# Banded output blocks moved ahead of their gates and stored ungated, with a second seven-product pair

## The chip, the cores and the metric

The kernel runs on one core of a Trainium2 chip. The metric is the device time of one execution in microseconds (us); less is better. The core has five engines with a queue of instructions each: PE multiplies matrices, ACT (ScalarE) and DVE (VectorE) work elementwise, POOL (GpSimd) mostly issues DMAs here, SP issues the loads of the weights. Each engine runs its instructions in an order that is fixed when the kernel is built; an instruction that waits holds up all that stand behind it on its engine. SBUF is the on-chip memory, PSUM the eight banks that PE writes its sums to, DRAM the memory outside.

## The reference, cut to what matters

One layer of a decoder trunk on 256 tokens of width 2048, all in float32. Three sub-steps matter: the projection of the gates, the two attention branches with an output projection each, and the merge.

```python
c_q, c_kv, k_r, q_s, k_s, v_s, gates = jnp.split(h @ w_in, offsets, axis=-1)
...
o_a = mla_attention(q_nope, q_rope, k_nope, k_rope, v)     # 16 heads, dense causal
o_b = swa_attention(q_s, k_s, v_s, swa_sinks, rel_table)   # 32 heads, banded, window 128
g = jax.nn.sigmoid(gates).reshape(B, S, 2, D_MODEL)
merged = g[:, :, 0] * (o_a @ w_o_mla) + g[:, :, 1] * (o_b @ w_o_swa)
y = merged @ w_out
```

The B branch (banded attention) ends in `sigmoid(gB) * (o_b @ w_o_swa)`; `gB` and `o_b @ w_o_swa` are two products of 256 x 2048 by 2048 x 2048. After the mixer come a norm, a gated convolutional feed-forward part and another norm, which the change does not touch.

## The kernel before, in words

**Products.** A float32 product is made of three passes on PE: operands are split into a high and a low part, and high by high, high by low and low by high are added up in PSUM (`mm3`, lines 174 to 177). Activations lie split in SBUF: the normed input in the eight tiles `xt` (family a, read through `XH` and `XL`), the banded attention's output in the eight tiles `ot` (family b, `OH` and `OL`). Weights come from DRAM through SP into raw tiles of 128 x 1024, and are split by `convert` (lines 134 to 145): ACT casts the high part `whi`, DVE subtracts for the low part `wlo`. Four such pairs of tiles form a ring, so the conversions run up to four tiles ahead of PE.

**A plain block.** `gemm` makes 256 tokens by 512 columns: eight weight tiles of two k-tiles each, for both halves of the tokens (t = 0, 1). After each weight tile `tick()` is called, which emits whatever was set for that step with `at(step, ...)`; so side work is spread over the steps of the main products.

**A pair.** `pair_gemm` makes two blocks (1024 columns) at once, from eight units of two k-tiles each. A unit `p` (plain) is eight products of 128 x 128 by 128 x 512. A unit `s` (`seven`) makes the same 2 x 2 x 2 block product with seven products, in the manner of Strassen and Winograd: it needs sums of the activations (`token_sums`) and sums of the weights (four subtractions of 512 columns on DVE), and its weight rows are loaded by POOL, not SP. Four sums `c` gather in four PSUM banks, and four others `q` in the other four; `kind` says which four are which. After the last unit `s` the `q` banks are combined into four tiles `d` in SBUF (`first_sums`, `more_sums`); to finish, `c` has to be added to `d`.

**The order around the change.** Behind the banded attention and the two latent projections come, one after another: gate block 0 (`gate_b(0)`, columns from `C_GB`), banded output block 0 (`out_b(0)`), gate blocks 1 and 2 as a pair (`gate_pair(1)`, order "psppspsp"), then output block 1, gate block 3, output blocks 2 and 3. `gate_b` leaves tanh of half of the gate in SBUF tiles `tb`; `out_b` multiplies (tanh + 1) by its PSUM sum on DVE (line 707) and POOL stores the gated product to `yb_d` in DRAM. The eight units of the latent attention (`mla_unit`) begin 26 steps after the gate pair and run beside output block 3 and the A gates; their outputs go into the b family again (`at_`), once the banded outputs are no longer needed. Then come the four blocks of the A gates, stored to `ta_d`.

**The merge** (lines 938 to 958) runs beside the four blocks of `wo_a`: POOL loads the stored A gate into `lta` (three buffers) and the gated B product into `lyb` (two buffers); DVE multiplies (tanh + 1) by the PSUM sum, adds the B product, and PE transposes the result (`m_cols`).

Other names: `stg` are four staging tiles of 128 x 512; `pacc` has four PSUM banks, `pss` and `pst` two each; `gr` are the two buffers for the rows that POOL loads, `gta` and `gtb` the sums of the weights.

Of the kernel before, what the change touches and what calls it, by code (L numbers as in the profile page):

```python
# [11 lines left out]
F32 = mybir.dt.float32  # L12
F32R = mybir.dt.float32r
# [3 lines left out]
ALU = mybir.AluOpType  # L17
AX = mybir.AxisListType

P = 128  # L20
D = 2048
S = 256
NT = 2
KT = D // P
# [17 lines left out]
def trunk_layer(ctx, tc, x, x_cols_in, conv_cols_in, g_mix_post, g_ffn_post, w_in, w_q, w_kv,  # L42
                sinks, rel, wo_a, wo_b, w_out, w_up, w_down, rope_tab, strip_sel, out):
    nc = tc.nc
    vec, act, pe, pool = nc.vector, nc.scalar, nc.tensor, nc.gpsimd
# [13 lines left out]
    def sb(pl, shape, name, dt=F32, tag=None, bufs=None):  # L59
        return pl.tile(shape, dt, name=name, tag=tag or name, **({"bufs": bufs} if bufs else {}))  # L60
# [41 lines left out]
    cnt = [0]  # L102
# [52 lines left out]
    now = [0]  # L155

    def at(t, *fs):
        steps[max(t, now[0])].extend(fs)
# [20 lines left out]
    def gemm(xh, xl, w, k0, nk, c0, n, split=None, extra=None, ps=None):  # L179

        kc = 1024 // n if n in (256, 512) else 2
        acc = new_acc("g", ps)
        todo = []
        cuts = list(range(0, nk, kc)) + [nk]
        for ci, (k, ke) in enumerate(zip(cuts[:-1], cuts[1:])):
            kk = ke - k
            src = w[(k0 + k) * P:(k0 + k + kk) * P, c0:c0 + n].rearrange("(a p) n -> p a n", p=P)
            hi, lo = wchunk(src, [kk, n], *(extra or {}).get(ci, ()))
            for j in range(kk):
                kt = k + j  # L190
# [85 lines left out]
    def token_sums(g, a, m, hi, lo):  # L276

        vec.tensor_tensor(a, g[:, 0:512], g[:, 512:1024], op=ALU.add)
        a11, a21, a12, a22 = (a[:, i * P:(i + 1) * P] for i in range(4))
        m1, m2, m3, m4 = (m[:, i * P:(i + 1) * P] for i in range(4))  # L280
        vec.tensor_tensor(m1, a21, a22, op=ALU.add)
        vec.tensor_tensor(m3, a11, a21, op=ALU.subtract)
        vec.tensor_tensor(m2, m1, a11, op=ALU.subtract)
        vec.tensor_tensor(m4, a12, m2, op=ALU.subtract)
        split_to(hi, lo, m)
        return [[x[:, i * P:(i + 1) * P] for x in (hi, lo)] for i in range(4)]
# [71 lines left out]
    xt = [slot("a", p) for p in range(8)]  # L358
# [139 lines left out]
    ot = [slot("b", p) for p in range(8)]  # L498
    OH, OL = pair_view(highs(ot)), pair_view(lows(ot))
# [113 lines left out]
    for g in range(4):  # L613
        acc = gemm(XH, XL, w_in, 0, KT, C_QS + 512 * g, 512)[0] if g else acc_q0
        swa_q(g, acc)
        b = now[0]
# [10 lines left out]
    stg = lambda name, n=512: sb(lpool, [P, n], name, tag="stg", bufs=STG)  # L627
# [36 lines left out]
    acc, _ = gemm(XH, XL, w_in, 0, KT, 0, 512)  # L664
# [25 lines left out]

    ta_d = dram.tile([4, NT, P, 512], F32, name="ta_d")
    yb_d = dram.tile([4, NT, P, 512], F32, name="yb_d")
    x2_d = dram.tile([NT, P, D], F32, name="x2_d")

    def gate_b(j):
        acc, _ = gemm(XH, XL, w_in, 0, KT, C_GB + 512 * j, 512)
        tb = []
        for t in range(NT):
            g = stg(f"tb{j}_{t}")
            act.activation(g, acc[t], AF.Tanh, scale=rh[:, t:t + 1])  # L700
            tb.append(g)
        return tb

    def out_b(j, tb, ps=None):
        acc, _ = gemm(OH, OL, wo_b, 0, KT, 512 * j, 512, ps=ps)
        for t in range(NT):
            vec.scalar_tensor_tensor(tb[t], tb[t], 1.0, acc[t], op0=ALU.add, op1=ALU.mult)
            pool.dma_start(yb_d[j, t], tb[t])

    es1.close()  # L710
    esb.close()
    esg, pg = open_pool("pg")
    xs = {}

    def x_sums(u):
        st = sb(pg, [P, 1024], f"xs{u}", F32R)
        a, m = (sb(pg, [P, 512], f"x{n}{u}", tag="x" + n, bufs=1) for n in "am")
        xs[u] = token_sums(xt[u].bitcast(F32), a, m, st[:, 0:512], st[:, 512:1024])

    def g_place():  # L720
        both = sb(pg, [P, D], f"gr{cnt[0]}", tag="gr", bufs=2)
        return both[:, 0:1024], both[:, 1024:2048]

    def gate_pair(j):
        d = [stg(f"tb{j + i}_{t}") for t in range(NT) for i in range(2)]
        c = pair_gemm("g", w_in, 0, C_GB + 512 * j, GATE_ORDER, lambda k, t: (XH(k)[:, t * P:(t + 1) * P], XL(k)[:, t * P:(t + 1) * P]),
                      lambda u: xs[u], 0, d, g_place, lambda: [sb(pg, [P, 1024], f"gt{n}{cnt[0]}", tag="gt" + n, bufs=2) for n in "ab"])
        def finish_gate(i):
            vec.tensor_tensor(d[i], d[i], c[i], op=ALU.add)
            act.activation(d[i], d[i], AF.Tanh, scale=rh[:, i // 2:i // 2 + 1])  # L730

        for n_, i in enumerate((0, 2, 1, 3)):
            at(now[0] + n_, lambda i=i: finish_gate(i))
        return [d[0], d[2]], [d[1], d[3]]

    tb = {0: gate_b(0)}
    for u in range(GATE_ORDER.count("s")):
        at(now[0] + 3 * u, lambda u=u: x_sums(u))
    out_b(0, tb[0], (pss, "s"))
    tb[1], tb[2] = gate_pair(1)  # L740
    esg.close()


    es2, p2 = open_pool("p2")
    CQH, CQL = pair_view(cqh), pair_view(cql)
    CKH, CKL = pair_view([ckh]), pair_view([ckl])
    ath, atl = [], []
    AH, AL = pair_view(ath), pair_view(atl)
    wq3 = w_q.rearrange("(k p) (h c) -> p k h c", p=P, c=192)
    xr_of = {}  # L750
# [133 lines left out]
        at(t0 + 6, lambda: pt(0), lambda: pt(1))  # L884
        at(t0 + 7, lambda: pv(0), lambda: pv(1))

    b = now[0] + 26
    for u in range(8):
        if u % 4 == 0:
            q_rope8(u // 4, b + 4 * u)  # L890
        mla_unit(u, b + 4 * u)

    for j in range(1, 4):
        out_b(j, tb[j], (pss, "s") if j == 1 else None)
        if j == 1:
            tb[3] = gate_b(3)
    at_ = [slot("b", p) for p in range(8)]
    ath[:], atl[:] = highs(at_), lows(at_)
    for j in range(4):
        acc, _ = gemm(XH, XL, w_in, 0, KT, C_GA + 512 * j, 512)  # L900
        for t in range(NT):
            g = stg(f"ta{j}_{t}")
# [35 lines left out]
    def merge_loads(j):  # L938
        ld = []
        for t in range(NT):  # L940
            a = sb(p4, [P, 512], f"lta{j}_{t}", tag="lta", bufs=3)
            b = sb(p4, [P, 512], f"lyb{j}_{t}", tag="lyb", bufs=2)
            pool.dma_start(a, ta_d[j, t])
            pool.dma_start(b, yb_d[j, t])
            ld.append((a, b))
        return ld

# [376 lines left out]

RING = 4
GATE_ORDER = "psppspsp"
B_ORDER = "pppsppspsp"
PAIR_ORDER = ("psppsppsppsp", "ppsppsppsppp")
XCUT = [0, 1, 2, 3, 4, 6, 8, 10, 12, 14, 16]
# [73 lines left out]
```

## Time and profile before

| | |
|---|---|
| time, median of 3 runs | 1468.54 us (1467.81 to 1469.31) |
| the profiled execution | 1470.05 us, of which the span is 1468.3 us |
| PE busy, share of the span | 99% |
| DVE, ACT, POOL | 73%, 57%, 4% |
| granted clock of PE | 0.998 of full speed |

The profile is of one execution. A row of the timeline or of a group names the line of the kernel, the engine, the operation and the tiles (out<-in); in a group the last figures are minimum, median and maximum in ns. "Idle before" in square brackets says how long the engine stood before the instruction and what released it. A product of 128 x 512 shows 0.39 us, but products are pipelined, so that one begins every 0.23 us. Some product records can be missing from a trace, so counts of products are a few per cent low.

### The profile page before, as it was taken

How to read it: one execution, taken by the hardware profiler on the slowest of the kernel's cores; microseconds unless marked ns; L12 is line 12 of the kernel's file. 1: busy time of each engine (PE TensorE's matmuls, PEld its weight loads, DVE VectorE, ACT ScalarE, POOL GpSimd, SP SyncE). 2: the span in 40 equal slices, each digit the busy share in tenths (PEclk: the TensorE clock that was granted, in tenths of full speed). 3: DMA queues.
4: the chain of work that ended last, by engine and by line, in shares of the span. 5: the costliest groups of instructions: out<-in, count | busy, mean ns of one | idle time of the engine just before them, and what ended most of it. 6: DMA issues, size and time to landing. Idle time of an engine off the chain costs nothing.

```text
span 1468.3 us, 20938 instructions
## 1 busy us (share of the span) xinstructions
PE 1456.9 (99%) x7576; PEld 1244.8 (85%) x7576; DVE 1067.2 (73%) x1881; ACT 830.5 (57%) x1372; POOL 64.9 (4%) x113
## 2 busy tenths in 40 slices
PE   9999999999999999999999999999999999999997
PEld 7888888888888888888888888888888888888886
DVE  7688896745667665555699976778776687677775
ACT  7588874543555554444566655555454565555453
POOL 0011110000000000000000000000000000000000
PEclk9999999999999999999999999999999999999999
DMA  8755376466655559756766666665656666667573
GB/s 297 211 164 167 108 259 192 162 212 200 191 156 160 164 163 334 226 184 212 225 205 185 188 193 193 187 187 187 218 174 213 198 187 189 187 197 233 163 237 129
DMA packets 149909, 287.60 MB, mean 196 GB/s; under 512 B 18428, under 2 KB 29597, under 8 KB 149677
## 3 DMA queue, kind: packets, MB, share of 16 engines
q1 hardware_dynamic: 141312, 256.80, 56.5%
q0 software_dynamic: 8400, 29.41, 6.4%
q8 instruction: 59, 0.97, 0.3%
q14 instruction: 46, 0.37, 0.1%
q10 hardware_dynamic: 92, 0.05, 0.0%
HBM read 277.79 MB, written 8.44 MB: 195 GB/s over the span
## 4 chain that ended last, share of the span: by engine, by line
PE 97%; DVE 2%; ACT 1%; issue 0%; DMA 0%; DVEq 0%; ACTq 0%
PE accg L175 13%; PE accg L177 13%; PE accg L176 13%; PE ub L1147 10%; PE ua L1147 10%; PE ua L1151 5%; PE ub L1151 5%; PE cd L177 2%; PE cd L175 2%; PE cd L176 2%; PE cdb L175 1%; PE cdb L177 1%; PE cdb L176 1%; PE mpo L875 1%; PE cg L176 1%; PE cg L177 1%
## 5 line engine op out<-in xcount | busy, mean ns | idle before, releaser
L144 DVE TENSOR_TENSOR wlo<-raw,whi 128x1024 fp32r<-128x1024 f32 (+2 forms) x476 | 576.3, 1214 | 282.5 <-ACT whi L143 275.2
L143 ACT CAST whi<-raw 128x1024 fp32r<-128x1024 f32 (+2 forms) x476 | 494.7, 1043 | 427.5 <-PE accg L177 172.3
L175 PE MATMUL accg<-whi,ahl 128*128 128x512 f32 (+1 forms) x480 | 187.9, 392 | 0.0
L177 PE MATMUL accg<-whi,ahl 128*128 128x512 f32 (+1 forms) x480 | 185.6, 387 | 0.0
L176 PE MATMUL accg<-wlo,ahl 128*128 128x512 f32 (+1 forms) x480 | 184.8, 385 | 0.0
L1147 PE MATMUL ua<-ahl,whi 128*128 128x512 f32 x640 | 154.6, 391 | 0.0
L1147 PE MATMUL ub<-ahl,whi 128*128 128x512 f32 x640 | 154.6, 391 | 0.0
L175 PE MATMUL accg<-whi,bhl 128*128 128x512 f32 x378 | 148.2, 392 | 0.0
L177 PE MATMUL accg<-whi,bhl 128*128 128x512 f32 x378 | 147.4, 390 | 0.0
L176 PE MATMUL accg<-wlo,bhl 128*128 128x512 f32 x378 | 147.3, 390 | 0.0
L1147 PEld LDWEIGHTS ub<-ahl,whi 128*128 128x128 f32 x640 | 117.5, 188 | 22.9 <-ACT cc L1045 0.2
L1147 PEld LDWEIGHTS ua<-ahl,whi 128*128 128x128 f32 x640 | 117.6, 188 | 22.7
L177 PEld LDWEIGHTS accg<-whi,ahl 128*128 128x128 f32 x480 | 90.1, 188 | 18.0
L176 PEld LDWEIGHTS accg<-wlo,ahl 128*128 128x128 f32 x480 | 90.3, 188 | 15.6
L175 PEld LDWEIGHTS accg<-whi,ahl 128*128 128x128 f32 x480 | 90.3, 188 | 15.5
L1151 PEld LDWEIGHTS ub<-ahl,wlo 128*128 128x128 f32 x640 | 82.2, 191 | 3.2
L1151 PEld LDWEIGHTS ua<-ahl,wlo 128*128 128x128 f32 x640 | 82.2, 191 | 3.1
L1151 PE MATMUL ua<-ahl,wlo 128*128 128x256 f32 x640 | 83.7, 283 | 0.0
L177 PEld LDWEIGHTS accg<-whi,bhl 128*128 128x128 f32 x378 | 71.0, 188 | 14.8
L176 PEld LDWEIGHTS accg<-wlo,bhl 128*128 128x128 f32 x378 | 71.0, 188 | 14.5
L1151 PE MATMUL ub<-ahl,wlo 128*128 128x256 f32 x640 | 83.2, 283 | 0.0
L175 PEld LDWEIGHTS accg<-whi,bhl 128*128 128x128 f32 x378 | 71.0, 188 | 14.3
(545 smaller groups left out, 2218.9 us busy)
## 6 DMA issues: line engine op xcount, KB each, us to landing
raw<-in_ffn_w_up_dram SPq DMA_DIRECT2D x176, 512.0 KB, 4.5
raw<-in_w_in_dram SPq DMA_DIRECT2D x105, 512.0 KB, 4.5
raw<-in_ffn_w_down_dram SPq DMA_DIRECT2D x68, 512.0 KB, 4.5
raw<-in_w_o_swa_dram SPq DMA_DIRECT2D x32, 512.0 KB, 4.4
raw<-in_w_o_mla_dram SPq DMA_DIRECT2D x32, 512.0 KB, 4.5
raw<-in_w_out_dram SPq DMA_DIRECT2D x32, 512.0 KB, 4.1
bias<-strip POOLq DMA_DIRECT2D x16, 256.0 KB, 4.4
raw<-in_mla_w_q_up_dram SPq DMA_DIRECT2D x32, 128.0 KB, 2.8
```

The lines of the kernel that those rows point to most:

```text
L143: act.copy(hi[:, a:b], raw[:, a:b])
L144: vec.tensor_tensor(lo[:, a:b], raw[:, a:b], hi[:, a:b].bitcast(F32), op=ALU.subtract)
L175: pe.matmul(o, ah, bh, start=start, stop=False)
L176: pe.matmul(o, ah, bl, start=False, stop=False)
L177: pe.matmul(o, al, bh, start=False, stop=stop)
L875: pe.matmul(o, w(t), p_[:, c], start=n == 0, stop=n == 5)
L1147: pe.matmul(acc[i], hi[:, c], hn[p][:, j * 512:(j + 1) * 512], start=p + j == 0, stop=stop)
L1151: pe.matmul(acc[i][:, 0:256], lo[:, c], hn[p][:, j * 512:j * 512 + 256], start=False, stop=False)
```

## The change

The banded output blocks no longer wait for their gates, since both go to DRAM by themselves: the output blocks ungated to `yb_d`, the tanh of the gates to a new `tb_d`. The order becomes output blocks 0 and 1 (plain), output blocks 2 and 3 as a pair (`out_pair(2)`), gate blocks 0 and 1 as a pair (`gate_pair(0)`), and then gate blocks 2 and 3 (plain) beside the latent attention, which begins 2 steps after the gate pair instead of 26. The `at_` tiles are taken right behind the gate pair.

Both pairs have three seven-product units. For them the sums of the activations are made for three tiles of `ot` and three of `xt`, spread over the steps of output blocks 0, 1 and the pair; the third sum of `xt` lies in the place of the first of `ot`.

The gate pair uses banks of the other kind than before (kind 1). In the output pair `d` is stored to `yb_d` first; then each `c` is copied by ACT to one of two buffers `yc` and added to what is stored by a DMA with an accumulating write.

The merge loads three tiles per token half (gate B, output B, gate A) with two buffers each, and multiplies (tanh + 1) by output B on DVE five steps into each block.

```diff
+    tb_d = dram.tile([4, NT, P, 512], F32, name="tb_d")
...
     def gate_b(j):
...
             act.activation(g, acc[t], AF.Tanh, scale=rh[:, t:t + 1])
-            tb.append(g)
-        return tb
-
-    def out_b(j, tb, ps=None):
-        acc, _ = gemm(OH, OL, wo_b, 0, KT, 512 * j, 512, ps=ps)
+            pool.dma_start(tb_d[j, t], g)
+
+    def out_b(j):
+        acc, _ = gemm(OH, OL, wo_b, 0, KT, 512 * j, 512, ps=(pss, "s") if j == 1 else None)
         for t in range(NT):
-            vec.scalar_tensor_tensor(tb[t], tb[t], 1.0, acc[t], op0=ALU.add, op1=ALU.mult)
-            pool.dma_start(yb_d[j, t], tb[t])
+            o = stg(f"yb{j}_{t}")
+            act.copy(o, acc[t])
+            pool.dma_start(yb_d[j, t], o)
...
+    def pair_sums(name, into, tiles, u):
+        st = sb(pg, [P, 1024], f"{name}{u}", F32R, tag="os0" if u == 2 and name == "xs" else f"{name}{u}")
+        a, m = (sb(pg, [P, 512], f"{name}{n}{u}", tag="x" + n, bufs=1) for n in "am")
+        into[u] = token_sums(tiles[u].bitcast(F32), a, m, st[:, 0:512], st[:, 512:1024])
...
     def gate_pair(j):
...
-                      lambda u: xs[u], 0, d, g_place, lambda: [sb(pg, [P, 1024], f"gt{n}{cnt[0]}", tag="gt" + n, bufs=2) for n in "ab"])
+                      lambda u: xs[u], 1, d, g_place, g_temps)
...
             act.activation(d[i], d[i], AF.Tanh, scale=rh[:, i // 2:i // 2 + 1])
+            pool.dma_start(tb_d[j + i % 2, i // 2], d[i])
...
+    def out_pair(j):
+        d = [stg(f"yu{j + i}_{t}") for t in range(NT) for i in range(2)]
+        c = pair_gemm("o", wo_b, 0, 512 * j, OUT_ORDER, lambda k, t: (OH(k)[:, t * P:(t + 1) * P], OL(k)[:, t * P:(t + 1) * P]),
+                      lambda u: os_[u], 0, d, g_place, g_temps)
+        for i in range(4):
+            pool.dma_start(yb_d[j + i % 2, i // 2], d[i])
+
+        def finish_out(i):
+            e = sb(pg, [P, 512], f"yc{i}", tag="yc", bufs=2)
+            act.copy(e, c[i])
+            pool.dma_start(yb_d[j + i % 2, i // 2], e, accum_op=ALU.add)
+
+        for i in range(4):
+            at(now[0] + i // 2, lambda i=i: finish_out(i))
+
+    for n_, u in ((6, 0), (9, 1), (12, 2)):
+        at(now[0] + n_, lambda u=u: pair_sums("os", os_, ot, u))
+    for n_, u in ((10, 0), (14, 1), (20, 2)):
+        at(now[0] + n_, lambda u=u: pair_sums("xs", xs, xt, u))
+    out_b(0)
+    out_b(1)
+    out_pair(2)
+    gate_pair(0)
     esg.close()
+    at_ = [slot("b", p) for p in range(8)]
+    ath, atl = highs(at_), lows(at_)
...
-    b = now[0] + 26
+    b = now[0] + 2
...
-    for j in range(1, 4):
-        out_b(j, tb[j], (pss, "s") if j == 1 else None)
-        if j == 1:
-            tb[3] = gate_b(3)
-    at_ = [slot("b", p) for p in range(8)]
-    ath[:], atl[:] = highs(at_), lows(at_)
+    for j in range(2, 4):
+        gate_b(j)
...
     def merge_loads(j):
         ld = []
         for t in range(NT):
-            a = sb(p4, [P, 512], f"lta{j}_{t}", tag="lta", bufs=3)
-            b = sb(p4, [P, 512], f"lyb{j}_{t}", tag="lyb", bufs=2)
-            pool.dma_start(a, ta_d[j, t])
-            pool.dma_start(b, yb_d[j, t])
+            a, g, b = (sb(p4, [P, 512], f"l{n}{j}_{t}", tag="l" + n, bufs=2) for n in ("ta", "tb", "yb"))
+            for dst, src in ((g, tb_d), (b, yb_d), (a, ta_d)):
+                pool.dma_start(dst, src[j, t])
+            at(now[0] + 5, lambda b=b, g=g: vec.scalar_tensor_tensor(b, g, 1.0, b, op0=ALU.add, op1=ALU.mult))
             ld.append((a, b))
...
 GATE_ORDER = "psppspsp"
+OUT_ORDER = "psppspsp"
```

More of the change, by code (lines that the diff above doesn't have):

```diff
@@ L696, in gate_b @@
         acc, _ = gemm(XH, XL, w_in, 0, KT, C_GB + 512 * j, 512)
-        tb = []
         for t in range(NT):
@@ L712, in trunk_layer @@
     esg, pg = open_pool("pg")
[L713 to L718, printed above, removed]
+    xs, os_ = {}, {}
+    def pair_sums(name, into, tiles, u):
+        st = sb(pg, [P, 1024], f"{name}{u}", F32R, tag="os0" if u == 2 and name == "xs" else f"{name}{u}")
+        a, m = (sb(pg, [P, 512], f"{name}{n}{u}", tag="x" + n, bufs=1) for n in "am")
+        into[u] = token_sums(tiles[u].bitcast(F32), a, m, st[:, 0:512], st[:, 512:1024])
     def g_place():
@@ L722, in g_place @@
         return both[:, 0:1024], both[:, 1024:2048]
+    g_temps = lambda: [sb(pg, [P, 1024], f"gt{n}{cnt[0]}", tag="gt" + n, bufs=2) for n in "ab"]
     def gate_pair(j):
@@ L730, in finish_gate @@
             act.activation(d[i], d[i], AF.Tanh, scale=rh[:, i // 2:i // 2 + 1])
[L732 to L740, printed above, removed]
+            pool.dma_start(tb_d[j + i % 2, i // 2], d[i])
+        for i in range(4):
+            at(now[0] + i // 2, lambda i=i: finish_gate(i))
+    def out_pair(j):
[8 more added lines that the diff above has]
+            pool.dma_start(yb_d[j + i % 2, i // 2], e, accum_op=ALU.add)
+        for i in range(4):
+            at(now[0] + i // 2, lambda i=i: finish_out(i))
[7 more added lines that the diff above has]
+    gate_pair(0)
     esg.close()
+    at_ = [slot("b", p) for p in range(8)]
+    ath, atl = highs(at_), lows(at_)
     es2, p2 = open_pool("p2")
@@ L746, in trunk_layer @@
     CKH, CKL = pair_view([ckh]), pair_view([ckl])
-    ath, atl = [], []
     AH, AL = pair_view(ath), pair_view(atl)
```

## The prediction

> **What bounds the kernel.** I read the page's head first, then its chain of waits.
>
> ```profile
> span 1468.3 us, 20938 instructions
> PE 1456.9 (99%) x7576; PEld 1244.8 (85%) x7576; DVE 1067.2 (73%) x1881; ACT 830.5 (57%) x1372; POOL 64.9 (4%) x113
> PE 97%; DVE 2%; ACT 1%; issue 0%; DMA 0%; DVEq 0%; ACTq 0%
> ```
>
> PE is busy for 99% of the span and makes 97% of the chain. Only fewer products, or a PE stall, can move the time. The second view is a table of stretches around the change; its columns are PE, PEld, DVE, ACT, POOL busy us (count), granted clock, DMA share, GB/s.
>
> ```profile
> 200.00:220.00 20.00, 20.00 (x92) 16.52 (x91) 20.00 (x50) 10.68 (x18) 2.51 (x5) 1.00 0.84 297
> 220.00:240.00 20.00, 20.00 (x90) 16.56 (x89) 12.90 (x15) 9.53 (x11) 0.00 (x0) 1.00 0.70 206
> 240.00:260.00 20.00, 20.00 (x89) 16.22 (x88) 14.16 (x16) 9.55 (x10) 2.17 (x4) 1.00 0.61 202
> 260.00:280.00 20.00, 20.00 (x89) 16.42 (x88) 11.92 (x12) 11.86 (x13) 0.00 (x0) 1.00 0.21 68
> 300.00:320.00 20.00, 20.00 (x90) 16.57 (x89) 10.57 (x10) 7.39 (x7) 1.10 (x2) 1.00 0.73 228
> ```
>
> PE has no hole and full clock, so there is no stall here to win back. A busy PE can still step slowly, so the third view is PE's timeline: first product of banded output block 0, first of the old gate pair, three marks in its first seven-product unit, the two steps that a late tile spoiled, and the first product behind the pair.
>
> ```profile
> 220.91 0.39 PE L175 MATMUL accg<-whi,bhl 128*128 128x512 f32 x1
> 242.67 0.39 PE L175 MATMUL cg<-whi,ahl 128*128 128x512 f32 x1
> ...
> 248.11 0.39 PE L175 MATMUL cg<-whi,ahl 128*128 128x512 f32 x1
> ...
> 250.89 0.39 PE L175 MATMUL qg<-whi,xs 128*128 128x512 f32 x1
> ...
> 251.60 0.40 PE L175 MATMUL qg<-whi,xs 128*128 128x512 f32 x1
> ...
> 252.98 0.39 PE L175 MATMUL cg<-whi,ahl 128*128 128x512 f32 x1
> 253.28 0.50 PE L176 MATMUL cg<-wlo,ahl 128*128 128x512 f32 x1
> 253.62 0.39 PE L177 MATMUL cg<-whi,ahl 128*128 128x512 f32 x1
> ...
> 284.68 0.39 PE L175 MATMUL accg<-whi,bhl 128*128 128x512 f32 x1
> ```
>
> A plain block is 96 products (16 k-tiles, 2 token halves, 3 products each) in 242.67 - 220.91 = 21.76 us: 0.2267 us a product, 2.72 us a weight tile (12 products). The durations of 0.39 overlap and are not the step.
>
> **Part 1, the products removed.** A plain unit of a pair is 2 x 2 x 2 x 3 = 24 products, a seven-product unit 21. Before, one pair (gates 1-2) has three such units; after, two pairs have six. So 9 products go, at most 9 x 0.2267 = 2.04 us. The old pair shows what such units really return: it lasts 284.68 - 242.67 = 42.01 us, two plain blocks 43.52, a gain of 1.51. The missing 0.53 is 0.19 at the late tile (252.98 to 253.62 is 0.64 for two steps of 0.227) and 0.34 in slightly slower steps with the summed operand. **I take -1.51**; bounds -2.04 and 0.
>
> **Part 2, VectorE's extra work.** The second pair adds, per seven-product unit, four subtractions and 1.5 more tile conversions, then four final sums, and three token sums.
>
> ```profile
> L232 DVE TENSOR_TENSOR gta<-gr x3: 678/685/692, 207.5 to 249.7; 128x512 f32<-128x512 f32 x3
> 240.15 1.05 ACT L143 CAST whi<-gr 128x1024 fp32r<-128x1024 f32 x1 [1.67 <-PE accg L177]
> 241.23 1.23 DVE L144 TENSOR_TENSOR wlo<-gr,whi 128x1024 fp32r<-128x1024 f32 x1 [1.49 <-ACT whi L143]
> ```
>
> That is 3 x (4 x 0.685 + 1.5 x 1.23) + 4 x 0.68 + 3 x 2.5 = 24 us; 2.5 for a token sum is an estimate (two additions of 0.685 and four on a quarter of the width). The stretch from banded block 0 to the end of the gate pair becomes 2 x 21.76 + 2 x 42.0 = 127.5 us. DVE has there what the first four stretches hold (59.0), 47.5 us of plain work at 10.57 per 20 (25), and the 24: 108 of 127.5, 0.85. In 200 to 220 it was full and PE did not stall. Cover in time: the low half above ends at 242.46 and its first product is at 248.11, so a DVE delay of 5.65 us is hidden in plain units. ACT ends at 241.20, 6.9 ahead. Cost 0; without that cover each 1.23 us conversion would be a stall. Gating only moves: the product of 1.28 for two tiles (L707 below) leaves the output blocks, ACT's copies (0.57) take its place, and eight products of 0.64 go to the merge.
>
> **Part 3, POOL's loads.** The even and odd rows of seven-product units go through two buffers and POOL's queue.
>
> ```profile
> 200.65 0.56 POOL L227 DMA_DIRECT2D gr<-in_w_in_dram  x1 [0.30 <-POOL bhl L605]
> ...
> 243.35 1.14 POOL L708 DMA_DIRECT2D yb_d<-tb  x2 [40.54 <-DVE tb L707]
> 244.55 0.54 POOL L227 DMA_DIRECT2D gr<-in_w_in_dram  x1
> 245.08 0.54 POOL L228 DMA_DIRECT2D gr<-in_w_in_dram  x1
> 242.37 1.28 DVE L707 SCALAR_TENSOR_TENSOR tb<-tb,accg 128x512 f32<-128x512 f32 x2
> 249.66 0.69 DVE L232 TENSOR_TENSOR gta<-gr 128x512 f32<-128x512 f32 x1 [1.77 <-DMA gr<-in_w_in_dram]
> ACT whi L143 <- DMA raw<-in_ffn_w_down_dram: 40.5, 23, 4.8
> ```
>
> Before, two of three loads ran 40 us ahead; the third left when a buffer came free, DVE stood 1.77 us at its subtraction with a conversion queued behind, and PE lost the 0.19 above. After, four loads are of that kind; one is in the 1.51, and the gate pair's first two are wanted more than 20 us after their buffers come free. **I take +0.2**; bounds 0 and 3.2 each (a wait of 4.8, the longest for a load in the table of waits, 3.0 more than 1.77).
>
> **Part 4, the accumulate chain, where the change adds waits.** At the end of the output pair (call it T; 284.68 in the old pair) four partial blocks are stored, the other four are copied by ACT into two buffers, and each is added to its stored part by a DMA. Copy 2 must wait until DMA 0 has landed, copy 3 until DMA 1 has, and DMA 1 until its own store has. Behind a waiting copy stand ACT's conversions; behind the DMAs on POOL the gate pair's third load and the stores of the gates. No row has an accumulating DMA; nearest are plain stores of the same 256 KB.
>
> ```profile
> 283.69 0.68 DVE L261 TENSOR_TENSOR tb<-tb,qg 128x512 f32<-128x512 f32 x1
> 288.36 0.68 DVE L729 TENSOR_TENSOR tb<-tb,cg 128x512 f32<-128x512 f32 x1
> 276.93 0.57 ACT L255 COPY tb<-qg 128x512 f32<-128x512 f32 x1
> DMA to landing us min/median/max: 2.3/4.2/6.0
> ```
>
> The first copy is done at about T - 1.3 (its bank closes nine products before T). At the median of 4.2, DMA 0 lands at T + 2.9, copy 2 ends at T + 3.5. Partial block 1 is final at 284.37 = T - 0.3; its store lands at T + 3.9, DMA 1 at T + 8.1, copy 3 ends at T + 8.7. PE wants copy 2's bank at T + 8.2 (250.89 - 242.67) and copy 3's at T + 8.9 (251.60 - 242.67). The plain tile of T + 10.3 (252.98) needs its cast to begin 2.3 us earlier, at T + 8.0: if that cast stands behind copy 3, PE loses 0.7. At 6.0 for each DMA copy 3 ends at T + 12.3 and PE loses 4.3. **I take +0.4**, near the median; bounds 0 and 4.3.
>
> The accumulate is also what the Trainium skill speaks against. "DMA: Bandwidth & Descriptors", section "Rules for kernel authors", says that an accumulating DMA must wait for the earlier DMA on the same bytes, the wait priced here. "Collectives: The Full Stack", section "The bandwidth ceiling: the fold count and why AG ≠ RS ≠ AR", says that an adding DMA reads two sources and so runs at about half the rate of a copy. No run here shows it; it is the first rival below.
>
> **Part 5, steps with cover.** The attention units start 3 tiles after the gate pair (T + 8.2) instead of 27. They need banks that the finishing additions free; the last one ended at 289.04, T + 4.4: 3.8 us of cover, and its price if that is gone is the lateness itself. They also end ten tiles before the last gate block instead of one:
>
> ```profile
> 548.96 0.68 DVE L318 TENSOR_TENSOR bhl<-mpo,bhl 128x512 fp32r<-128x512 f32 x1
> 574.82 1.28 DVE L955 SCALAR_TENSOR_TENSOR lta<-lta,accg 128x512 f32<-128x512 f32 x2
> 584.55 1.06 POOL L943 DMA_DIRECT2D lta<-ta_d  x2 [6.41 <-PE mT L935]
> ```
>
> In the merge six loads per block replace four and the A-gate buffers go from three to two, so that the second token half's loads queue behind the load that waits for the transposes (584.55). Its B product lands at 584.55 + 2 x 0.54 + 4.2 = 589.8 (6.0: 591.6) and is due five tiles into the block, which follows the first merge product of the one before: 574.82 + 13.6 = 588.4. DVE may stand 1.4 to 3.2 us, under 5.65. Cost 0; without cover 3 x 3.2 = 9.6. The output block that loses eight tiles of distance from the attention before it is covered too: DVE and POOL finish its operands as PE reads only the first.
>
> **Sum.** -1.51 + 0.2 + 0.4 = -0.9. The profiled execution took 1470.05 (span 1468.3 and 1.75 around it), 1.5 over the median of the runs; it would become 1469.1. From the median 1468.54 it is **1467.6 us**. A measurement of this kernel tells 0.2% (2.9 us) from no change; even all 2.04 us stay inside.
>
> **Rivals.**
> (a) *Accumulating DMAs at twice a store*, 8.4 us. DMA 1 lands at T + 12.3, copy 3 ends at T + 12.9, 4.9 behind T + 8.0: -1.51 + 0.2 + 4.9 = +3.6, 1472.1. It decides from 12.0 us for store and accumulate together (a stall of 4.25). For it: three DMAs in a row behind the last sum and only two buffers. Against: the DMA share there was 0.21.
> (b) *Late row loads in the seven-product units*: two of the four loads wait 4.8 us: 2 x 3.2 - 1.51 + 0.4 = +5.3, 1473.8. For it: the 1.77 already cost something. Against: loads leave earlier than they are wanted.
> (c) *The gain is given back exactly*, by small waits in part 4 and the merge of 1.5 us: 1468.5. That would be the change not doing what it says in time.
> (d) *Full 2.04 and another order of the attention's small stalls* worth 1 us more: 1465.5. Against: the stretch is full.
>
> **How the numbers follow.** Forecast (1466.3 to 1468.3) 0.52, (a) 0.22, (b) 0.08, (c) 0.10, (d) 0.08. Faster is (d) and a little of the forecast, 0.09; slower is (a) and (b), 0.30; the rest, 0.61, is within 0.2%. The range leaves out (b) and half of (a) and (d): 1465.5 to 1472.2.
>
> **What would show it.** Right: 9 fewer 128x512 products; both pairs about 42.0 us from first product to the next stage's; copies 2 and 3 on ACT with waits for DMA of under 2 us; gaps of under 0.5 us in PE's steps. Wrong: a PE gap of several us 8 to 13 us into the gate pair with the accumulate as releaser (a); gaps inside seven-product units released by DVE subtractions that wait for row loads (b); gaps in the merge.

## The result, and the profile after

The changed kernel takes **1472.65 us** (median of 12 runs, 1470.67 to 1473.66), the kernel before beside it 1468.56 (12 runs, 1467.81 to 1469.31). The ratio is 1.0027 with a 95% interval of 1.0019 to 1.0035: slower by 4.1 us. The forecast was 1467.6, and its range ended at 1472.2, 0.45 us short of the result. The profiled execution took 1472.53 us.

The head of the page and the chain of waits of the kernel after:

```profile
span 1470.4 us, 21023 instructions
...
PE 1457.3 (99%) x7567; PEld 1243.8 (85%) x7567; DVE 1087.3 (74%) x1921; ACT 840.4 (57%) x1390; POOL 80.3 (5%) x139
...
PE 93%; DVE 3%; DMA 1%; issue 1%; ACT 1%; POOL 0%; DVEq 0%; ACTq 0%; POOLq 0%
```

7567 products are listed, 9 fewer than before: part 1 of the prediction. VectorE gained 20.1 us (24 were counted) and stays far from being the bound. But the chain now leaves PE for 7% of the span instead of 3%, through VectorE, a DMA and ACT. PE's timeline of the kernel after shows where (start, duration, engine, line, tiles; in brackets idle time and releaser). The first row is the first product of the output pair, the second the first of the gate pair, the last the first product behind it:

```profile
241.52 0.39 PE L175 MATMUL co<-whi,bhl 128*128 128x512 f32 x1
...
283.74 0.39 PE L175 MATMUL cg<-whi,ahl 128*128 128x512 f32 x1
...
291.04 0.40 PE L177 MATMUL qg<-whi,ahl 128*128 128x512 f32 x1
291.55 0.50 PE L175 MATMUL qg<-whi,xs 128*128 128x512 f32 x1
292.81 0.50 PE L176 MATMUL qg<-wlo,xs 128*128 128x512 f32 x1 [0.77 <-DVE wlo L144]
...
293.83 0.40 PE L177 MATMUL qg<-whi,xs 128*128 128x512 f32 x1
296.12 0.50 PE L175 MATMUL qg<-whi,xs 128*128 128x512 f32 x1 [1.89 <-ACT yc L748]
...
297.06 0.63 PE L175 MATMUL cg<-whi,ahl 128*128 128x512 f32 x1
...
300.05 0.44 PE L176 MATMUL cg<-wlo,ahl 128*128 128x512 f32 x1
...
330.71 0.39 PE L175 MATMUL accg<-whi,ahl 128*128 128x512 f32 x1
```

Stages are measured from their first product to the next stage's first product:

| stage, us | before | after |
|---|---|---|
| output blocks 2 and 3 | 43.52 (two plain blocks) | 42.22 |
| the gate pair | 42.01 | 46.97 |
| sum | 85.53 | 89.19 |

The new output pair returns 1.30, but the gate pair takes 4.96 more than the old one. The sum is +3.66 of the 4.1 that the runs show. (The two profiled spans differ by 2.1 only: the profiled execution of before begins this part 1.15 later, at 198.38 where the other is at 197.23, and behind it the kernel after is 0.4 shorter.) Against the 41.80 us that the same pair takes when nothing is late (an experiment below), 46.97 holds 5.17 us too much. The rows tell how they divide, a step being 0.23: 0.28 and 1.03 at 291.55 and 292.81, where a converted weight tile is late; 2.06 at 296.12, where a PSUM bank is late; and seven steps of 0.427 from 297.06 to 300.05, 1.4 in all. The other 0.4 is spread in small amounts around them.

What is late is seen on ACT, VectorE and POOL. ACT's timeline of the kernel after:

```profile
282.17 1.06 ACT L748 COPY yc<-co 128x512 f32<-128x512 f32 x2
...
289.96 0.59 ACT L748 COPY yc<-co 128x512 f32<-128x512 f32 x1 [5.40 <-DMA yb_d<-yc]
290.44 1.05 ACT L143 CAST whi<-gta 128x1024 fp32r<-128x1024 f32 x1
291.39 1.05 ACT L143 CAST whi<-gtb 128x1024 fp32r<-128x1024 f32 x1
295.48 0.58 ACT L748 COPY yc<-co 128x512 f32<-128x512 f32 x1 [3.04 <-DMA yb_d<-yc]
```

The same stretch on VectorE, one row:

```profile
291.53 1.23 DVE L144 TENSOR_TENSOR wlo<-gta,whi 128x1024 fp32r<-128x1024 f32 x1 [4.34 <-ACT whi L143]
```

and on POOL:

```profile
283.06 0.90 POOL L749 DMA_DIRECT2D yb_d<-yc  x1 [0.42 <-ACT yc L748]
283.82 1.23 POOL L744 DMA_DIRECT2D yb_d<-yu  x2
286.16 0.54 POOL L227 DMA_DIRECT2D gr<-in_w_in_dram  x1 [1.11 <-DVE wlo L144]
291.43 1.75 POOL L749 DMA_DIRECT2D yb_d<-yc  x2 [4.73 <-DMA yb_d<-yu]
292.54 1.19 POOL L228 DMA_DIRECT2D gr<-in_w_in_dram  x1
```

Read together: copies 0 and 1 fill the two `yc` buffers. Copy 2 stands 5.40 us on ACT until DMA 0, issued at 283.06, has landed. Behind it stand the casts of `gta` and `gtb`, the weight sums of the first seven-product unit. VectorE waits 4.34 for the cast of `gta`, and PE for VectorE's low half of it. On POOL, DMA 1 waits 4.73 for the store of its own partial block; copy 3 waits for DMA 1, and PE for copy 3's bank. The even row load of the third unit leaves at 286.16, but the odd one stands behind the accumulating DMAs until 292.54. Landing times (median of each group), from the table of DMA issues:

```profile
yb_d<-yu POOLq DMA_DIRECT2D x4, 256.0 KB, 5.9
...
yb_d<-yc POOLq DMA_DIRECT2D x4, 256.0 KB, 4.8
...
yb_d<-yb POOLq DMA_DIRECT2D x4, 256.0 KB, 3.5
```

and the stretches (PE, PEld, DVE, ACT, POOL busy us and counts, granted clock, DMA share, GB/s):

```profile
284.00:291.00 7.00, 7.00 (x32) 5.79 (x31) 3.15 (x5) 1.60 (x3) 1.59 (x3) 1.00 1.01 309
291.00:297.00 6.00, 3.24 (x11) 1.82 (x10) 3.06 (x3) 2.96 (x5) 2.95 (x4) 0.98 0.77 137
297.00:300.10 3.10, 3.10 (x9) 2.37 (x8) 3.06 (x3) 2.85 (x4) 0.20 (x1) 0.50 1.03 213
```

The DMA engines are full in the 7 us in which three stores, an accumulating DMA and loads of rows and weights are in flight. A store of this size lands in 3.5 us elsewhere (`yb`); the two that begin at 283.82 take 6.7 each, and DMA 0 takes 6.8. After the hole the granted clock is 0.50 for 3 us: the seven slow steps.

### The profile page after: what moved, and what is told of

It reads as the page before. It is cut to its first block, busy times and chain, and to the rows that moved or that the text cites. A ratio compares the mean times of both kernels' runs of the same rounds, so it can differ in the third digit from the quotient of the medians.

```text
span 1470.4 us, 21023 instructions
## 1 busy us (share of the span) xinstructions
PE 1457.3 (99%) x7567; PEld 1243.8 (85%) x7567; DVE 1087.3 (74%) x1921; ACT 840.4 (57%) x1390; POOL 80.3 (5%) x139
## 4 chain that ended last, share of the span: by engine, by line
PE 93%; DVE 3%; DMA 1%; issue 1%; ACT 1%; POOL 0%; DVEq 0%; ACTq 0%; POOLq 0%
PE accg L175 12%; PE accg L177 12%; PE accg L176 12%; PE ub L1165 10%; PE ua L1165 10%; PE ub L1169 5%; PE ua L1169 5%; PE cd L177 2%; PE cd L175 2%; PE cd L176 2%; DVE wlo L144 1%; PE cdb L176 1%; PE cdb L177 1%; PE cdb L175 1%; PE mpo L897 1%
## 5 line engine op out<-in xcount | busy, mean ns | idle before, releaser
L144 DVE TENSOR_TENSOR wlo<-raw,whi 128x1024 fp32r<-128x1024 f32 (+2 forms) x470 | 568.6, 1215 | 242.2 <-ACT whi L143 237.2
L143 ACT CAST whi<-raw 128x1024 fp32r<-128x1024 f32 (+2 forms) x470 | 487.3, 1042 | 390.5 <-PE accg L177 139.4
L175 PE MATMUL accg<-whi,bhl 128*128 128x512 f32 x314 | 123.3, 393 | 0.0
L177 PE MATMUL accg<-whi,bhl 128*128 128x512 f32 x314 | 122.5, 390 | 0.0
L176 PE MATMUL accg<-wlo,bhl 128*128 128x512 f32 x314 | 122.4, 390 | 0.0
L177 PEld LDWEIGHTS accg<-whi,bhl 128*128 128x128 f32 x314 | 59.0, 188 | 12.2
L176 PEld LDWEIGHTS accg<-wlo,bhl 128*128 128x128 f32 x314 | 59.0, 188 | 12.0
L175 PEld LDWEIGHTS accg<-whi,bhl 128*128 128x128 f32 x314 | 59.0, 188 | 12.0
```

The source lines that it names most:

```text
L143: act.copy(hi[:, a:b], raw[:, a:b])
L144: vec.tensor_tensor(lo[:, a:b], raw[:, a:b], hi[:, a:b].bitcast(F32), op=ALU.subtract)
L175: pe.matmul(o, ah, bh, start=start, stop=False)
L176: pe.matmul(o, ah, bl, start=False, stop=False)
L177: pe.matmul(o, al, bh, start=False, stop=stop)
```

## The experiments

Each is an edit of the changed kernel; each ratio is to runs of the kernel before beside it (medians 1468.54 to 1468.79). The theory: DMAs that wait in order hold ACT's copies and so PE (part 4). The rivals: the traffic alone makes other loads late; the accumulating DMA is itself slow; the new order, the stores or the merge cost the time.

**Four buffers for the copies.** Copies 2 and 3 go into the two scratch tiles of the token sums, so that no copy waits for a DMA.

```diff
-            e = sb(pg, [P, 512], f"yc{i}", tag="yc", bufs=2)
+            e = sb(pg, [P, 512], f"yc{i}", tag=("yc", "yc", "xa", "xm")[i], bufs=2 if i < 2 else 1)
```

> The four copies of the finished sums get a tile each instead of sharing two; accumulating DMAs, stores and all else stay. Theory (the copies wait for a buffer, and ScalarE's casts and two PSUM banks wait behind them): no copy waits for a DMA, the hole of 5.2 us 7 to 16 us into the gate pair falls under 0.5, no half clock there, time 1467 to 1468.4. Rival one (the gate pair's row loads and VectorE's subtractions are late, 12 seven-product tiles in a row): the hole stays over 3 us, 1470 to 1473. Rival two (the DMA engines are full there, so every load is late): a hole of 2 us or more remains, 1469.5 to 1472.

Measured: 1472.1 us (8 runs, 1471.03 to 1474.74), ratio 1.0026 (1.0016 to 1.0037). ACT's, POOL's and VectorE's timelines of this kernel:

```profile
281.85 2.35 ACT L748 COPY yc<-co 128x512 f32<-128x512 f32 x4
```

```profile
287.31 0.88 POOL L749 DMA_DIRECT2D yb_d<-yc  x1 [2.59 <-issue]
287.88 0.86 POOL L227 DMA_DIRECT2D gr<-in_w_in_dram  x1
291.02 1.75 POOL L749 DMA_DIRECT2D yb_d<-yc  x2 [2.28 <-DMA yb_d<-yu]
292.13 1.20 POOL L228 DMA_DIRECT2D gr<-in_w_in_dram  x1
```

```profile
293.87 0.69 DVE L232 TENSOR_TENSOR gta<-gr 128x512 f32<-128x512 f32 x1 [5.23 <-DMA gr<-in_w_in_dram]
294.48 1.22 DVE L144 TENSOR_TENSOR wlo<-gtb,whi 128x1024 fp32r<-128x1024 f32 x1
```

The copies run back to back and nothing is won: the gate pair takes 46.71. Between the accumulating DMAs stands the even row load of a later unit; it leaves at 287.88, behind one of them, and lands 6 us later. VectorE reaches the subtraction that needs it 5.23 us too early, and the conversion of `gtb`, which PE needs now, is queued behind it: one hole of PE of 3.01 us. With ACT free, the rows are what is late.

**The second sum added in SBUF.** VectorE adds `c` to `d` and one store per block follows: no copies, no accumulating DMA.

```diff
-        for i in range(4):
+
+        def finish_out(i):
+            vec.tensor_tensor(d[i], d[i], c[i], op=ALU.add)
             pool.dma_start(yb_d[j + i % 2, i // 2], d[i])
-
-        def finish_out(i):
-            e = sb(pg, [P, 512], f"yc{i}", tag="yc", bufs=2)
-            act.copy(e, c[i])
-            pool.dma_start(yb_d[j + i % 2, i // 2], e, accum_op=ALU.add)
```

> The output pair is finished as the gate pair is: VectorE adds the four finished sums to the partial blocks in SBUF, and four stores follow; no copies, no accumulating DMA, 1 MB less to DRAM. Theory: no hole, time 1466.8 to 1468, at or slightly under the run with four copies, with the VectorE additions (four of 0.68 us) hidden. Rival one: the hole stays, 1470 to 1473. Rival two: some of it goes with the 1 MB, 1468.5 to 1470.

Measured: 1467.72 (11 runs, 1467.1 to 1470.71), ratio 1.0000 (0.9991 to 1.0009). The gate pair takes 42.15: all of the loss goes with the accumulate chain, its copies, DMAs and traffic together. The two pairs still take 0.7 more than 2 x 41.80. Rows of the table of waits in this kernel (engine, tile, line, releaser: us in all, times, longest) show for what:

```profile
DVE gta L232 <- DMA gr<-in_w_in_dram: 3.2, 3, 1.8
...
DVE gta L232 <- DMA gr<-in_w_o_swa_dram: 1.3, 1, 1.3
```

**A plain second store in the accumulating DMA's place.** The copies go to a tensor of their own, so that the kernel leaves the addition out; DMAs and buffers stay as many.

```diff
-            pool.dma_start(yb_d[j + i % 2, i // 2], e, accum_op=ALU.add)
+            pool.dma_start(yc_d[j + i % 2, i // 2], e)
```

> The four copies keep their two buffers but go to DRAM by plain stores to a place of their own; left out is the addition to the stored partial blocks, so output blocks 2 and 3 lack half their terms. This keeps the wait for a buffer and takes away both the accumulation and the wait of each such DMA for its own earlier store. If the two buffers alone make the hole: the third copy still waits 4 to 6 us, the fourth now at the same time, time 1469 to 1471. If the accumulation and its wait on the earlier store make it: under 1468.3. Rival one: unchanged, 1472 to 1473.

Measured: 1470.03 (11 runs, 1467.95 to 1471.66), ratio 1.0010 (1.0001 to 1.0019). These stores need not wait for the first ones, and the gate pair takes 42.02. They land in 4.8 us in the median, as the accumulating DMAs do, so adding doesn't double the time. But the one that copy 2 waits for lands in 4.9 where the accumulating one took 6.8 (5.7 to 7.2 in the six other kernels that have it), and the two plain stores beside it in 5.1 and 5.0 where they took 6.7. The DMA engines are as full there (share 1.02) and move 362 GB/s instead of 309. So part of the longer flight may be the addition's; but the weight loads ahead of the burst were also issued 1.2 us earlier here, counted from the gate pair's first product, and no run separates the two. In the profiled execution, one of the slower ones at 1471.44, a row load was late in the output pair instead (46.05 us), which is rival (b); the time lies in the expected range, but for another reason than the expected one. VectorE's and ACT's rows:

```profile
277.38 0.69 DVE L232 TENSOR_TENSOR gta<-gr 128x512 f32<-128x512 f32 x1 [4.46 <-DMA gr<-in_w_in_dram]
```

```profile
291.84 0.59 ACT L749 COPY yc<-co 128x512 f32<-128x512 f32 x1 [3.42 <-DMA yc_d<-yc]
```

The wait for a buffer is there as well, 3.42, but short enough to be hidden.

**The first seven-product unit one unit later**, so that its banks and tiles are wanted later.

```diff
-GATE_ORDER = "psppspsp"
+GATE_ORDER = "ppspspsp"
```

> The gate pair's first seven-product unit moves from the second to the third place; the same work, the same DMAs and waits on ScalarE and GpSimd. Theory: the two PSUM banks and the casts are wanted 5.4 us later, so the copies still wait for DMAs by 3 to 6 us each, and PE loses 0 to 1.5 us instead of 5.2: 1467.3 to 1469. If the copies held up ScalarE whatever PE does next: 1470 to 1472.

Measured: 1477.26 (5 runs, 1476.12 to 1478.54), ratio 1.0059 (1.0047 to 1.0072): a miss. The copies wait as long as before (5.32 and 3.85); POOL, and in its turn VectorE, show the rest:

```profile
298.38 0.56 POOL L227 DMA_DIRECT2D gr<-in_w_in_dram  x1 [0.40 <-DVE wlo L144]
```

```profile
303.62 0.69 DVE L232 TENSOR_TENSOR gta<-gr 128x512 f32<-128x512 f32 x1 [4.06 <-DMA gr<-in_w_in_dram]
...
305.45 1.22 DVE L144 TENSOR_TENSOR wlo<-gtb,whi 128x1024 fp32r<-128x1024 f32 x1
```

More slack for the first unit is less for the next: the third unit's rows can be asked for only when the first unit's are converted. These casts stood on ACT behind copies 2 and 3, so the load leaves at 298.38 and its rows come too late; the first unit's `gtb` is again queued behind the subtraction that wants them (gate pair 51.56). Slack at one consumer doesn't help while the queues are held.

**Four buffers, and the gate pair's rows on SP's queue**, past POOL's waits.

```diff
-            pool.dma_start(even, row(2 * u))
-            pool.dma_start(odd, row(2 * u + 1))
+            q_ = nc.sync if name == "g" else pool
+            q_.dma_start(even, row(2 * u))
+            q_.dma_start(odd, row(2 * u + 1))
...
-            e = sb(pg, [P, 512], f"yc{i}", tag="yc", bufs=2)
+            e = sb(pg, [P, 512], f"yc{i}", tag=("yc", "yc", "xa", "xm")[i], bufs=2 if i < 2 else 1)
```

> Four tiles for the four copies, and the gate pair's even and odd rows are loaded by SyncE instead of GpSimd, so that no row load stands behind an accumulating DMA. Theory (the accumulate chain holds up two queues, ScalarE through the copies and GpSimd with the row loads behind it, and each alone makes a hole of 3 us or more at VectorE or ScalarE): with both freed VectorE waits under 2 us for the third unit's rows, no hole over 0.5 us, 1467 to 1468.4, like the addition in SBUF (1467.7). Rival (the accumulating DMAs and stores fill the DMA engines, so row loads land late on any queue): VectorE still waits 3 to 5 us for rows, 1470 to 1472.

Measured: 1472.63 (7 runs, 1470.54 to 1475.56), ratio 1.0027 (1.0016 to 1.0038): a miss. Its profiled execution, the second fastest of them at 1470.73, has a gate pair of 44.19. VectorE waits less, but waits, 2.79 for the even rows and 1.05 for the odd:

```profile
291.20 0.69 DVE L233 TENSOR_TENSOR gta<-gr 128x512 f32<-128x512 f32 x1 [2.79 <-DMA gr<-in_w_in_dram]
```

With two row buffers the load can't be asked for until the first unit's rows are converted (285.8), and then it flies among the stores: 5.3 us for the even rows and 7.9 for the odd, where the earlier row loads of this pair took 3.9 to 5.1. POOL's queue was only a part of its lateness; the buffer is the other part.

**Two buffers, and the rows on SP** (the edit of the loads alone).

```diff
-            pool.dma_start(even, row(2 * u))
-            pool.dma_start(odd, row(2 * u + 1))
+            q_ = nc.sync if name == "g" else pool
+            q_.dma_start(even, row(2 * u))
+            q_.dma_start(odd, row(2 * u + 1))
```

> As changed (two tiles for four copies), but the gate pair's rows are loaded by SyncE. Theory: ScalarE still waits at the third and fourth copy (3 to 5 us each), the hole at 7 to 13 us into the gate pair stays at 3 to 5 us, 1470.5 to 1472.7. Rival (only the row loads behind the accumulating DMAs cost): 1467 to 1468.4.

Measured: 1476.19 (5 runs, 1474.83 to 1478.41), ratio 1.0052 (1.0038 to 1.0066); the gate pair takes 49.63. ACT:

```profile
288.84 0.59 ACT L749 COPY yc<-co 128x512 f32<-128x512 f32 x1 [5.60 <-DMA yb_d<-yc]
289.32 1.05 ACT L143 CAST whi<-gta 128x1024 fp32r<-128x1024 f32 x1
294.14 0.59 ACT L749 COPY yc<-co 128x512 f32<-128x512 f32 x1 [3.77 <-DMA yb_d<-yc]
294.62 1.05 ACT L143 CAST whi<-gtb 128x1024 fp32r<-128x1024 f32 x1
```

Rows in time don't help while ACT is held. Here the cast of `gtb` stands behind copy 3 instead of ahead of it, so that PE waits for it too; that goes with the kernel being 3.5 us slower than the changed one. With other queues the order on ACT came out different.

**No output pair**: output blocks 2 and 3 plain and no sums of their activations, everything else of the change kept.

```diff
...
-    out_pair(2)
+    out_b(2)
+    out_b(3)
```

> The new order, the ungated stores and the merge as changed, but output blocks 2 and 3 are two plain blocks; only the gate pair has seven-product units, so the number of products is that of before. Theory: order, stores and merge cost nothing: 1468.2 to 1469.0, the time of before; with the addition in SBUF at 1467.7 the second pair is then worth 0.8. Rival (the moved attention units or the merge cost time): over 1469.5.

Measured: 1467.74 (11 runs, 1467.24 to 1468.95), ratio 0.9994 (0.9985 to 1.0003). The gate pair takes 41.80. So the order, the ungated stores and the merge's six loads per block cost nothing that can be measured, as part 5 had it.

**Both holds removed**: the addition in SBUF as above, and three row buffers instead of two (the second sum of `xt` takes the place of the second of `ot`, and the sums are made at other steps).

```diff
...
-        both = sb(pg, [P, D], f"gr{cnt[0]}", tag="gr", bufs=2)
+        both = sb(pg, [P, D], f"gr{cnt[0]}", tag="gr", bufs=3)
...
-    for n_, u in ((10, 0), (14, 1), (20, 2)):
+    for n_, u in ((10, 0), (20, 2), (26, 1)):
```

> The addition in SBUF, and a third buffer for the even and odd rows, so that each unit's rows are asked for one unit earlier; the second sum of the input lies in the place of the second sum of the banded output and is made later. If late row loads (VectorE waits of 0.7 to 1.8 us in the run without it) take what the second pair should give: 1466.3 to 1467.2, with a smaller spread of runs. If not: 1467.5 to 1468.

Measured: **1466.46** (11 runs, 1465.7 to 1467.68), ratio 0.9984 (0.9976 to 0.9993): 2.3 us faster than the kernel before, and faster than the changed one. PE's timeline of it, first products of both pairs and of the next stage:

```profile
241.83 0.39 PE L175 MATMUL co<-whi,bhl 128*128 128x512 f32 x1
...
283.63 0.39 PE L175 MATMUL cg<-whi,ahl 128*128 128x512 f32 x1
...
325.43 0.39 PE L175 MATMUL accg<-whi,ahl 128*128 128x512 f32 x1
```

Each pair takes 41.80, 1.72 less than two plain blocks. Against the kernel without the output pair (1467.74) the second pair is now worth 1.3 us; with two row buffers (1467.72) it was worth nothing that can be measured.

**Three row buffers, two buffers for the copies** (the scratch tiles), accumulating DMAs kept: only the hold on ACT is left.

```diff
-        both = sb(pg, [P, D], f"gr{cnt[0]}", tag="gr", bufs=2)
+        both = sb(pg, [P, D], f"gr{cnt[0]}", tag="gr", bufs=3)
...
-            e = sb(pg, [P, 512], f"yc{i}", tag="yc", bufs=2)
+            e = sb(pg, [P, 512], f"yc{i}", tag=("xa", "xm")[i % 2], bufs=1)
...
```

> As changed with two tiles for the four copies, and the third buffer for the row loads. Theory: ScalarE still waits 4 to 6 us at the third copy and 3 to 4 us at the fourth; the hole at 7 to 13 us into the gate pair stays, 3.5 to 7 us, 1470 to 1474. Rival (the rows alone): 1466.3 to 1468.

Measured: 1472.63 (7 runs, 1470.56 to 1473.71), ratio 1.0028 (1.0017 to 1.0038), the changed kernel's own time; the gate pair takes 49.09 in the profiled execution, at 1473.6 one of the slowest. The table of waits has no wait of VectorE for rows, only

```profile
ACT yc L748 <- DMA yb_d<-yc: 9.3, 2, 5.2
```

**Three row buffers, four copies.** Copies 0 and 1 go into the scratch tiles, 2 and 3 into the halves of the third sum's tile of `ot`, which is free by then.

```diff
...
-            e = sb(pg, [P, 512], f"yc{i}", tag="yc", bufs=2)
+            if i % 2 == 0:
+                yc[:] = [sb(pg, [P, 1024], f"yc{i}", tag="os2")[:, k * 512:(k + 1) * 512] for k in range(2)] if i == 2 else [sb(pg, [P, 512], f"yc{n}", tag="x" + n, bufs=1) for n in "am"]
+            e = yc[i % 2]
```

> As changed, accumulating DMAs and all, but with a tile for each of the four copies and a third buffer for the row loads, so that ScalarE waits for no DMA and the third unit's rows are asked for ahead of the accumulating DMAs. Theory (the DMAs cost only through who waits for them: copies on ScalarE, row loads behind them on GpSimd and VectorE's subtraction on the rows): no hole over 0.5 us, gate pair 41.8 to 42.3 us, 1466.3 to 1467.8. Rival (the DMA engines are full and the weight tiles come late too): a hole of 2 us or more, 1469 to 1472.

Measured: 1469.48 (11 runs, 1468.2 to 1470.44), ratio 1.0005 (0.9996 to 1.0014). Not as clean as it was meant: the last copy still waits once, on ACT:

```profile
290.72 0.59 ACT L752 COPY yc<-co 128x512 f32<-128x512 f32 x1 [3.87 <-DMA yb_d<-yc]
291.20 1.05 ACT L143 CAST whi<-gtb 128x1024 fp32r<-128x1024 f32 x1
```

It waits for the DMA of copy 2, which reads the other half (issued at 285.89, landed 4.8 us later): the two halves count as one tile. One wait of 3.87 with a cast behind it: the pair takes 43.93, 2.13 over 41.80, and the median is 3.0 over that of the kernel with both holds removed.

**Traffic, with two row buffers and with three.** To the kernels with the addition in SBUF come four stores more and four DMAs that add onto them, on POOL, 12 in all; no copy waits for any.

```diff
             pool.dma_start(yb_d[j + i % 2, i // 2], d[i])
+            pool.dma_start(yc_d[j + i % 2, i // 2], d[i])
+            pool.dma_start(yc_d[j + i % 2, i // 2], d[i], accum_op=ALU.add)
```

With two:

> The addition in SBUF with two row buffers, and beside each of its four stores one more store of the same tile to a place of its own and an accumulating DMA onto that: twelve DMAs where there were four, and nobody on ScalarE or VectorE waits for them; the added place is read by no one. Theory: the gate pair's third row load stands behind the waiting accumulating DMAs on GpSimd and VectorE waits 3 to 6 us for it; hole 2 to 5 us, 1470 to 1473. Rival (traffic and queue cost nothing where no copy waits): 1467 to 1468.

With three:

> The same twelve DMAs with three row buffers, so that the row loads go ahead of them. Theory: no one waits for them, no hole over 0.5 us, 1466 to 1467.5. Rival (full DMA engines make the weight tiles or rows late all the same): 1468.5 or more.

Measured: 1474.79 with two (5 runs, 1472.64 to 1476.34; ratio 1.0045, 1.0031 to 1.0059) and 1466.59 with three (11 runs, 1465.96 to 1467.51; ratio 0.9987, 0.9978 to 0.9995). Waits of the first, and of the second with a stretch of it (columns as above):

```profile
DVE gta L232 <- DMA gr<-in_w_in_dram: 10.9, 3, 8.6
```

```profile
POOL yc_d L749 <- DMA yc_d<-yu: 5.3, 3, 2.2
```

```profile
292.00:300.00 8.00, 8.00 (x37) 6.62 (x36) 6.92 (x8) 3.78 (x4) 1.75 (x2) 1.00 1.03 285
```

In the second the DMA engines are as full as in the changed kernel (1.03), POOL waits 5.3 us for landings, and PE has no hole and full clock; both pairs take 41.80. So this traffic costs nothing where nobody in a hurry is queued behind it (1466.59 against 1466.46). With two buffers the third unit's even rows are queued on POOL behind it until 295.32 and then fly 10.0 us in the full DMA engines; the time is 8 us longer, above both expectations.

## Why the prediction was wrong, by its steps

**The step that failed** is part 4, the accumulate chain, taken at +0.4. Against a pair with nothing late it costs 5.17, and the kernel without it is back at the time of before (1467.72). With 5.17 in its place the prediction's own sum, -1.51 + 0.2 + 5.17, gives 1472.4. The chain works through two holds, one behind the other: copies that wait on ACT ahead of casts, and row loads that leave late and fly among the chain's DMAs:

| kernel | ACT held | rows held | us |
|---|---|---|---|
| the change | yes | hidden behind ACT | 1472.65 |
| four copy buffers | no | yes | 1472.1 |
| four copy buffers, rows on SP's queue | no | late all the same | 1472.63 |
| three row buffers, two copy buffers | yes | no | 1472.63 |
| three row buffers, four copies | once | no | 1469.48 |
| addition in SBUF, two row buffers | no | short waits | 1467.72 |
| the same with 12 DMAs | no | yes | 1474.79 |
| addition in SBUF, three row buffers | no | no | 1466.46 |
| the same with 12 DMAs | no | no | 1466.59 |

Removing either alone wins nothing; removing both wins 6 us. Both are off only in kernels that leave the copies out as well; with four copies and three row buffers one wait on ACT was left.

**The term was mis-sized for three reasons.** First, the duration. I took the median of 4.2 from a trace in which the DMA share was 0.2 to 0.8 and kept 6.0 as the bound. That line holds the eight stores to `yb_d` together with the eight loads of the merge; the stores alone landed in 3.9 and at most 5.1, so the range was not one of stores. The stretch that the change makes has a share of 1.01: DMA 0 landed 6.8 us after its issue (283.06 to 289.86, when copy 2's wait ends), the store of partial block 1 took 6.7 (one of the two that begin at 283.82; POOL goes on at 291.43), DMA 1 4.0. Copy 3 ended at T + 12.3 (296.06 - 283.74), the bound's own figure, for which the prediction gave a loss of 4.3. Second, who is behind. I asked which bank and which plain tile PE would want, and priced one cast behind copy 3; the casts of `gta` and `gtb` stood behind copy 2. The queue of POOL was named with the third row load in it, but not priced. Third, the 1.4 us at half clock after the hole were not in the sum.

**Rival (a)** put the stall in the right place and its total at 1472.1, but for a reason that the runs don't bear out: that the total fits is luck. It had the accumulating DMA at 8.4; in the changed kernel they took 4.0 to 6.8, where the plain stores beside them took up to 6.7. The wait for one's own store and landing times in full DMA engines made the delay; what share of these the adding has stays open (4.9 for the first plain second store). Only in the two traffic kernels did accumulating DMAs take 8.6 to 9.5 us, the last two of four in each; in the one with two buffers the row loads beside them were as slow (10.0 and 9.4). What "Collectives: The Full Stack", section "The bandwidth ceiling: the fold count and why AG ≠ RS ≠ AR", of the Trainium skill says of adding DMAs (about half the rate of a copy; the section speaks of the ring steps of collectives) is not borne out by the landing times of the changed kernel. What "DMA: Bandwidth & Descriptors", section "Rules for kernel authors", says of the wait for the earlier DMA on the same bytes is borne out: 4.73 us on POOL.

**Rival (b)**, late row loads, is small in the changed kernel and became large wherever ACT's hold was taken away and the chain's DMAs were kept with two row buffers (a wait of 5.23 with four copy buffers, 8.6 with the added traffic), and once in an output pair (46.05). With the addition in SBUF two buffers cost 0.38 and 0.35 a pair (42.18 and 42.15, against 41.80 with three buffers), where part 3 said 0.2 for both.

**Right** were the nine products and the return of a pair (1.51 forecast, 1.30 measured beside a late load, 1.72 with none late, of at most 2.04); VectorE's cover (its waits are for others, not for itself); and part 5, since without the output pair the rest of the change takes 1467.74. The place to look for a wrong forecast was also right: a gap 8 to 13 us into the gate pair. It began at T + 7.8 and lasted until T + 12.4.

**Open**: the holds cost about the same alone as together, in one stretch of one kernel; how much each would cost at other due times was not measured, nor how much longer the adding itself makes the burst. It is not known either why the order on ACT of a cast and a copy differs between two builds.

## What to carry to other kernels

Price a wait for a DMA by the slowest landing with the DMA engines full, since the burst that the change issues is itself what fills them, and then list everything that is queued behind the waiting instruction on each in-order engine, the next pair's loads and conversions above all. If removing one such wait wins nothing, look for a second that was hidden behind it before dropping the theory. Buffers one deeper (copies, rows) or an addition on chip cost little against a wait in a queue that PE depends on.

## What the runs showed of the hardware

The granted clock fell to 0.50 for some 3 us after short holes of PE: 0.77 and 1.89 us idle within 4 us (the change), and 2.25 alone (0.50 from 279.8 to 282.9, in the output pair of the plain second store). It stayed at 1.00 after 0.58 and 1.23 within 4 us (four buffers with the rows on SP), and after 1.74, 1.71 and 0.78 within 7 us (the traffic with two buffers), of which the last two lie within 4 us and add up to 2.49, more than the 2.25. So the sum of the holes alone doesn't decide here. The seven slow steps of the change cost 1.4 us on top of its holes. "TensorE: Matmul & The Clock Gate", section "What's actually happening", of the Trainium skill has the drop to half after an idle window of about 3.4 us; of the holes here only one was that long (5.45, the later seven-product unit), and the clock fell after shorter ones too.

The issue of an accumulating DMA holds POOL for 0.85 to 1.19 us in the changed kernel, where the plain second stores in its place took 0.54. Whether the adding does that is not shown: a plain row load right behind one took 0.86 too (four copy buffers). The spread of runs grew from 1.5 us (before) to 3 us (the change) and 5 (four buffers, rows on SP); where nobody waits for the landings it is 1.6 again (the second traffic kernel). Varying landing times in the full stretch would explain it, but only one execution of each kernel was profiled.
